# Two-layer decoder trunk on one Trainium2 core: retrieval routing decoded two heads at a time, its lists in SBUF and its scratch in PSUM, with operand splits queued behind the norm and 16 chunks in the queries

## The chip, the core and the metric

The kernel runs on one core of one Trainium2 chip. The metric is the device time of one execution in microseconds (us). A core has engines with queues of their own, each of which runs its instructions in order: PE (matrix products, into PSUM), DVE (vector work), ACT (functions and casts), POOL (a second, slower vector engine) and SP (which issues transfers). SBUF is the working memory. PSUM is a small memory of eight banks to which PE writes. An instruction that needs the result of another engine waits on a semaphore, and whatever stands behind it on its own engine waits too.

## The reference

Each of two layers mixes tokens, attends to 256 memory tokens, and then runs a retrieval over 16384 single-neuron experts, each step followed by a residual and a layer norm. The change lies in the retrieval (512 tokens, 8 heads, 128 keys on each of two sides, 16 kept):

```python
qry = (x @ wq).reshape(B, S, PEER_HEADS, PEER_QDIM)
s1 = jnp.einsum('bshc,nc->bshn', qry[..., :PEER_HALF], k1)
s2 = jnp.einsum('bshc,nc->bshn', qry[..., PEER_HALF:], k2)
v1, i1 = lax.top_k(s1, PEER_TOPK)
v2, i2 = lax.top_k(s2, PEER_TOPK)
cand = (v1[..., :, None] + v2[..., None, :]).reshape(...)
sc, ci = lax.top_k(cand, PEER_TOPK)
expert = take(i1, ci // 16) * N_KEYS + take(i2, ci % 16)
gate = softmax(sc)
out = einsum(gate * gelu(einsum(x, u[expert])), v[expert])
```

## The kernel before

The sum over chosen experts is not gathered for the first three of the four blocks of 128 tokens (384 tokens). There the kernel computes all 16384 experts, in 128 **chunks** of 128 experts. A chunk on the first side is 24 products of 128 x 384 on PE (`Peer.u_chunk`), followed on ACT by a gelu (L1219). On the second side (`Peer.dense`) its activations are multiplied by a dense row of gates (`coef`, L1240) and six blocks of products are added up in PSUM. The fourth block of tokens is gathered row by row beside that. Full precision products are made of three passes (`mm3`, L230 to L232) over a high and a low part of each operand: `split` casts the high part on ACT (L225) and subtracts for the low part on DVE or POOL (L226).

In each layer five stages touch the change.

- **Norm.** `out_proj_ln` ends with the layer norm of the last token block. `rstd` (L296) takes a logarithm and an exponential on ACT (L299, L300) and some short DVE work, `layer_norm` scales on DVE (L327), and PE transposes the result (L281). The splits of the first weights and chunks stand in the queues of ACT and POOL around it.
- **Queries** (`queries`, L777). For each head PE projects the queries (`proj`), then runs one chunk, then the scores against the keys (L806), which ACT copies to SBUF (L807). From the second head on, the low parts of the weights are subtracted on POOL (`weng`). DVE meanwhile runs `route` (L868): for each head two times four lists of 128 scores, then four lists of 80 candidates. Each list is a call of `top16`: a maximum of eight (L858), its indices (L860), a replacement (L862), and the same for the next eight (L864, L866). Sixteen short operations and three long ones (L922, L925, L929) then decode the expert's number. The best values of the first side, all indices and most of the decode's operands lie in one PSUM bank (`ps`); a second bank (`pi`) takes the shifts. `main` and `routes` are generators, and `weave` writes their code in turn by the costs that they yield. A scheduler sets the final order on each engine.
- **QUERY** is 20: after the last scores PE goes on with chunks, and the low part of a chunk is subtracted on POOL up to that number, on DVE behind it.
- **Gate rows** (`gate_rows`, L937, called from `body`, L1083). Routing must be complete. For each of three token blocks PE transposes the experts' numbers (L950) and the gates (L954). For every four tokens DVE (and ACT in one of four) makes one-hot rows (L965, L970), POOL multiplies them by the gates (L967), PE multiplies the two (L974), ACT copies the result (L975), and SP sends the rows to memory (L981). Chunks are woven in: EARLY (3) before, then AHEAD - c - LATE less EARLY, where c counts the chunks already done, and LATE (5) behind the last row. Thirty chunks (AHEAD) are thus complete when the dense stage begins.
- **Dense.** It reads the gate rows back from memory, and PE's products follow each other until the end of the layer.

`al` gives a tile of SBUF from an arena of pages; a page that was used before makes its new user wait for the old one. `bank()` hands out the eight PSUM banks in the same manner. `peer.more` allots rows for the activations.

Of the kernel before, what the change touches and what calls it, by code (L numbers as in the profile page):

```python
# [21 lines left out]
NT = S // 128  # L22
# [10 lines left out]
DT = 384  # L33
GT = 32
AHEAD = 30
QUERY = 20
EARLY = 3
LATE = 5
PF = 3
TAIL = 4  # L40
ROWS = 7
# [140 lines left out]
class K:  # L182
# [113 lines left out]
    def rstd(self, out, var, scale, eps, t, v):  # L296

        nc = self.nc
        nc.scalar.activation(t, var, AF.Ln, scale=scale, bias=eps)  # L299
        nc.scalar.activation(t, t, AF.Exp, scale=-0.5)  # L300
        nc.vector.tensor_scalar(v, var, scale, eps, op0=OP.mult, op1=OP.add)
        nc.vector.tensor_mul(out, t, t)
        nc.vector.tensor_mul(out, out, v)
        nc.vector.tensor_scalar(out, out, -0.5, 1.5, op0=OP.mult, op1=OP.add)
        nc.vector.tensor_mul(out, out, t)
# [471 lines left out]
    def queries(self, l, xT, peer, X, xs):  # L777

        nc, a = self.nc, self.a
        kk = self.al((2, NK))  # L780
        nc.sync.dma_start(kk, a["keysT"][l])
        sc = {}

        def proj(h):
            w = self.weights() if h else self.weights(0)
            q = []
            for b in ([0, 1],) if h == 0 else ([0], [1]):
                bks = [self.bank() for _ in b]
                emit(self.fm_proj(w, b, xT, bks, None if h else 0))
                for bk in bks:  # L790
                    q.append(self.al((S,)))
                    nc.scalar.copy(q[-1], bk)
            if h == 0:
                self.wahead(2, 1)
                self.weng = nc.gpsimd
            w.free()
            return q

        def scores(h, q):
            sc[h] = self.al((NT, 2, NK))  # L800
            for t2 in range(2):
                bk = self.bank((128, 2, 2, NK))
                for tt in range(2):
                    o = slice((2 * t2 + tt) * 128, (2 * t2 + tt + 1) * 128)
                    for i in range(2):
                        nc.tensor.matmul(bk[:, tt, i, :], q[i][:, o], kk[:, i, :], start=True, stop=True)  # L806
                nc.scalar.copy(sc[h][:, 2 * t2:2 * t2 + 2], bk)  # L807
            self.fr(*q)

        def main():  # L810

            for h in range(1, H):
                q = proj(h)
                yield 10.9
                peer.u_chunk()
                yield 4.2
                scores(h, q)
                yield 1.7
                for _ in range(1 if h < H - 1 else QUERY - peer.c):
                    peer.u_chunk()  # L820
                    yield 4.2

        def routes():
            for h in range(H):
# [43 lines left out]
    def route(self, h, sc, ga, ef):  # L868


        nc = self.nc
        ta, tb, sh = self.al((512,)), self.al((NT, NC)), self.al((2 * NT, 4, TOPK))
        ps, pi = self.bank(), self.bank((128, 2 * NT, 4, TOPK))

        def part(t, o, *s):
            return t[:, o:o + int(np.prod(s))].rearrange(
                "p (t n) -> p t n" if len(s) == 2 else "p (t i n) -> p t i n", t=s[0],
                **({} if len(s) == 2 else dict(i=s[1])))

# [3 lines left out]
        m = part(ps, 256, NT, TOPK).bitcast(U32)  # L883
        r = part(ps, 320, NT, 2, TOPK)
        e1 = part(ps, 448, NT, TOPK).bitcast(U32)
        v2 = part(ta, 0, NT, TOPK)
        i8 = ta[:, 64:96].bitcast(U8)
        q = part(ta, 128, NT, TOPK).bitcast(U32)
        d = part(ta, 192, NT, TOPK)
        e2 = part(ta, 256, NT, TOPK).bitcast(U32)  # L890
        tv = ga[:, :, h, :]
        for i, v in enumerate((v1, v2)):
            self.top16([(sc[:, t, i, :], v[:, t, :], ix[:, t, i, :]) for t in range(NT)])
            yield 4.3
        self.fr(sc)

        nc.vector.tensor_copy(i8, ps[:, 64:192].bitcast(U32))

        s1 = [128, NT, 7, 8]
        nc.vector.tensor_add(tb[:, :, 0:16], v1[:, :, 0:1].to_broadcast([128, NT, 16]), v2)  # L900
        nc.vector.tensor_add(tb[:, :, 16:72].rearrange("p t (a b) -> p t a b", a=7),
                             v1[:, :, 1:8, None].to_broadcast(s1), v2[:, :, None, 0:8].to_broadcast(s1))
        nc.vector.tensor_add(tb[:, :, 72:80], v1[:, :, 8:16], v2[:, :, 0:1].to_broadcast([128, NT, 8]))
        yield 0.8
        self.top16([(tb[:, t, :], tv[:, t, :], ti[:, t, :]) for t in range(NT)])
        yield 3


        nc.vector.tensor_scalar(q, ti, 120, None, op0=OP.bitwise_and)
# [6 lines left out]
        nc.vector.tensor_add(r[:, :, 1, :], r[:, :, 1, :], d)  # L916


        shape = [128, 2 * NT, 4, TOPK]
        si, su = pi.bitcast(I32), sh.bitcast(U32)  # L920
        r = r.rearrange("p t i k -> p (t i) k")
        nc.vector.tensor_sub(si, self.lanes[:, None, :, None].to_broadcast(shape),  # L922
                             r[:, :, None, :].to_broadcast(shape))
# [4 lines left out]
        en = part(ps, 320, NT, 2, TOPK).bitcast(U32)  # L928
        nc.vector.tensor_reduce(en.rearrange("p t i k -> p (t i) k"), su.rearrange("p a w k -> p a k w"),  # L929
                                axis=AX.X, op=OP.max)  # L930
        nc.vector.tensor_scalar(e1, en[:, :, 0, :], 24, None, op0=OP.logical_shift_right)
        nc.vector.tensor_scalar(e2, en[:, :, 1, :], 24, None, op0=OP.logical_shift_right)
        nc.vector.scalar_tensor_tensor(ef[:, :, h, :], e1, float(NK), e2, op0=OP.mult, op1=OP.add)
        self.fr(ta, tb, sh)
        yield 4

    def gate_rows(self, tb, ga, ef, dram, stages):  # L937

# [144 lines left out]
    def body(self, out):  # L1083
# [19 lines left out]
        for l in range(L):  # L1103
# [272 lines left out]
```

## Time and profile before

| | value |
|---|---|
| median of 3 runs | 3532.67 us (3530.05 to 3540.63) |
| the profiled execution | 3532.14 us, of which the span is 3530.4 us |
| PE busy | 3417.4 us (97% of the span) |
| DVE busy | 2570.0 us (73%) |
| ACT busy | 1431.2 us (41%) |
| POOL busy | 1136.0 us (32%) |

The span runs from the first to the last instruction of the execution. Both layers have the same form: in the first the queries lie at 485 to 690 us, the gate rows at 690 to 810 us and the dense stage at 810 to 1690 us; in the second at 2245, 2450 and 2565 us. Below, a timeline row gives the start, the length, the engine, the line, the operation with its tiles and shape, and in brackets how long the engine had been idle before and what ended that. PE's records of one product overlap the next, so one reads starts, not lengths, where records follow each other.

### The profile page before, as it was taken

The page shows a single profiled execution, that of the slowest core. Times are in us where ns is not written, and L with a number is a line of the kernel's source. Part 1 is how long each engine was busy: PE and PEld are TensorE (multiplying, and loading weights), DVE is VectorE, ACT ScalarE, POOL GpSimd, SP SyncE. Part 2 cuts the span into 40 slices and gives each one's busy share as a digit, 9 for nine tenths or more (in the row PEclk, how much of TensorE's full clock was granted, in tenths as well). Part 3 has the DMA queues.
Part 4 walks back from the last instruction along what each step waited for, and adds up shares of the span by engine and source line. Part 5 has one row for each costly group of instructions (what it writes and reads, how often), then busy time and mean ns, then how long its engine had stood idle before and what let it go on. Part 6 is the DMA issues. An engine that isn't in the chain of part 4 may idle for free.

```text
span 3530.4 us, 49767 instructions
## 1 busy us (share of the span) xinstructions
PE 3417.4 (97%) x18546; PEld 3022.8 (86%) x18546; DVE 2570.0 (73%) x5006; ACT 1431.2 (41%) x2411; POOL 1136.0 (32%) x821
## 2 busy tenths in 40 slices
PE   9999999899999999999999999997899999999998
PEld 7679789789999999998876788897899999999987
DVE  4676469996777777778746754699867777777787
ACT  5553332483333333334346532324833333333332
POOL 0110043283444343345101100433824443434450
PEclk9999999999999999999999999999999999999999
DMA  3242232259988888889612322322598888888894
GB/s 147 61 137 77 91 108 77 79 234 346 317 297 293 300 296 295 302 294 339 216 36 70 131 73 92 108 67 90 245 348 311 295 305 289 304 296 291 302 327 149
DMA packets 280579, 744.42 MB, mean 211 GB/s; under 512 B 21648, under 2 KB 120464, under 8 KB 277264
## 3 DMA queue, kind: packets, MB, share of 16 engines
q1 hardware_dynamic: 206608, 472.76, 38.8%
q0 software_dynamic: 73728, 268.47, 21.8%
q8 instruction: 146, 2.39, 0.3%
q14 instruction: 97, 0.79, 0.1%
HBM read 685.57 MB, written 55.57 MB: 210 GB/s over the span
## 4 chain that ended last, share of the span: by engine, by line
PE 81%; DVE 12%; issue 3%; ACT 2%; POOL 1%; DMA 1%; DVEq 0%; SPq 0%; POOLq 0%; ACTq 0%
PE bk L230 24%; PE bk L231 23%; PE bk L232 23%; PE bk L974 5%; DVE bk L866 2%; DVE bk L860 1%; DVE plain L862 1%; PE bk L771 1%; DVE parts L226 1%; PE bk L742 1%; PE bk L572 1%; PE bk L528 1%; DVE plain L327 1%; DVE plain L858 1%; DVE plain L864 1%
## 5 line engine op out<-in xcount | busy, mean ns | idle before, releaser
L232 PE MATMUL bk<-parts 128*128 128x384 f32 (+1 forms) x3746 | 1350.6, 361 | 4.2 <-DVE parts L226 4.2
L231 PE MATMUL bk<-parts 128*128 128x384 f32 (+2 forms) x3752 | 1333.3, 355 | 0.0
L230 PE MATMUL bk<-parts 128*128 128x512 f32 (+1 forms) x3554 | 1276.1, 359 | 0.7 <-ACT parts L225 0.7
L226 DVE TENSOR_TENSOR parts<-plain,parts 128x1024 fp32r<-128x1024 f32 (+2 forms) x747 | 730.0, 985 | 445.4 <-issue 363.9
L225 ACT CAST parts<-plain 128x1024 fp32r<-128x1024 f32 (+2 forms) x787 | 656.2, 863 | 717.1 <-PE bk L231 629.0
L232 PEld LDWEIGHTS bk<-parts 128*128 128x128 f32 x3746 | 704.1, 188 | 73.3 <-DVE parts L226 6.6
L231 PEld LDWEIGHTS bk<-parts 128*128 128x128 f32 x3752 | 706.5, 188 | 63.6
L230 PEld LDWEIGHTS bk<-parts 128*128 128x128 f32 x3554 | 669.0, 188 | 63.4 <-ACT parts L225 1.1
L1002 POOL DMA_INDIRECT mid<-peer_v,plain x256 | 377.4, 1474 | 494.4 <-DVE mid L1025 377.4
L1002 POOL DMA_INDIRECT mid<-peer_u,plain x256 | 363.9, 1421 | 530.6 <-DVE plain L1037 378.7
L230 PE MATMUL bk<-parts,mid 128*128 128x512 f32 (+2 forms) x912 | 349.5, 386 | 11.1 <-ACT mid L225 7.6
L1219 ACT ACTIVATE plain<-bk 128x384 f32<-128x384 f32 x256 | 125.4, 490 | 571.4 <-PE bk L232 571.4
L1037 DVE SCALAR_TENSOR_TENSOR plain<-mid,plain 128x1024 f32<-128x1024 f32 x256 | 329.0, 1285 | 3.4
L231 PE MATMUL bk<-parts,mid 128*128 128x512 f32 (+2 forms) x912 | 325.8, 358 | 1.5 <-DVE parts L226 1.5
L1025 DVE SCALAR_TENSOR_TENSOR mid<-mid,plain 128x1024 f32<-128x1024 f32 x256 | 303.4, 1220 | 3.3 <-DMA mid<-peer_u,plain 3.3
L226 POOL TENSOR_TENSOR parts<-plain,parts 128x1024 fp32r<-128x1024 f32 x40 | 99.4, 2490 | 526.6 <-ACT parts L225 507.8
L232 PE MATMUL bk<-parts,mid 128*128 128x512 f32 (+2 forms) x720 | 252.0, 351 | 0.0
L225 ACT CAST mid<-plain 128x1024 fp32r<-128x1024 f32 x163 | 168.9, 1038 | 193.3 <-PE bk L232 84.7
L230 PE MATMUL bk<-mid,parts 128*128 128x256 f32 (+1 forms) x798 | 237.0, 297 | 0.0
L967 POOL TENSOR_TENSOR mid<-mid,mid 128x512 f32<-128x512 f32 x192 | 192.6, 1040 | 115.6 <-DVE mid L965 114.8
L232 PE MATMUL bk<-mid,parts 128*128 128x256 f32 (+1 forms) x798 | 228.9, 287 | 0.0
L230 PEld LDWEIGHTS bk<-parts,mid 128*128 128x128 f32 (+1 forms) x912 | 171.8, 189 | 56.6 <-issue 17.8
(237 smaller groups left out, 3855.2 us busy)
## 6 DMA issues: line engine op xcount, KB each, us to landing
plain<-peer_uT SPq DMA_DIRECT2D x256, 512.0 KB, 4.7
plain<-peer_v SPq DMA_DIRECT2D x256, 512.0 KB, 5.4
plain<-gates SPq DMA_DIRECT2D x64, 768.0 KB, 9.3
gates<-plain SPq DMA_DIRECT2D x22, 2048.0 KB, 6.3
plain<-w_in SPq DMA_DIRECT2D x44, 512.0 KB, 5.4
plain<-xa_wkv SPq DMA_DIRECT2D x32, 512.0 KB, 3.8
plain<-peer_wq SPq DMA_DIRECT2D x32, 512.0 KB, 4.1
plain<-w_out SPq DMA_DIRECT2D x16, 512.0 KB, 5.0
```

What stands on the lines that cost most here:

```text
L225: nc.scalar.copy(hi, src)
L226: return (eng or nc.vector).tensor_sub(lo, src, hi.bitcast(F32))
L230: nc.tensor.matmul(out, lt[0], rt[0], start=first, stop=False)
L231: nc.tensor.matmul(out, lt[0], rt[1], start=False, stop=False)
L232: nc.tensor.matmul(out, lt[1], rt[0], start=False, stop=last)
L866: nc.vector.max_index(i[:, 8:16], v[:, 8:16], s)
L967: nc.gpsimd.tensor_mul(o[:, 0], o[:, 0], st[:, 2, t:t + 4, None].to_broadcast([128, 4, NK]))
L974: nc.tensor.matmul(bk[:, k, :], o[:, 1, k, :], o[:, 0, k, :], start=True, stop=True)
L1002: nc.gpsimd.indirect_dma_start(out=t, out_offset=None, in_=self.a[n], in_offset=bass.IndirectOffsetOnAxis(ap=ei[:, s:s + 1], axis=0))
L1025: nc.vector.scalar_tensor_tensor(u, u, 1.0, x, op0=OP.mult, op1=OP.mult, accum_out=act[:, s:s + 1])
L1037: nc.vector.scalar_tensor_tensor(acc, v, act[:, s:s + 1], acc, op0=OP.mult, op1=OP.add)
L1219: k.nc.scalar.activation(g, bk[:, :DT], AF.Gelu)
```

## The change

Three things are altered.

1. `route` handles two heads in one call. The best values of both sides, all indices, and the operands q and d lie in one SBUF tile `ta` of 1024 columns; m, r and the decoded entries in a PSUM bank; the shifts in two PSUM banks, in place. Each decode operation covers 128 columns per partition where it covered 64, save the long ones, which are done once for each half.
2. The first ahead-of-time split of the next weights (`wahead` in `proj(0)`) and `peer.preload`, which loads three chunks and splits chunk 0, are issued with an `issue_after` on the last exponential of the norm.
3. QUERY goes from 20 to 16 and LATE from 5 to 4. Eleven steps of `main` are written before the weave, where it was three, with other costs in the weave; two of the activation rows are allotted later.

```diff
-QUERY = 20
+QUERY = 16
-LATE = 5
+LATE = 4
...
-        nc.scalar.activation(t, t, AF.Exp, scale=-0.5)
+        self.last_exp = nc.scalar.activation(t, t, AF.Exp, scale=-0.5)
...
             if h == 0:
-                self.wahead(2, 1)
+                with self.tc.issue_after(norm.ins):
+                    self.wahead(2, 1)
...
-            for h in range(H):
-                yield from self.route(h, sc.pop(h), peer.ga, peer.ef)
+            for h in range(0, H, 2):
+                yield from self.route(h, sc, peer.ga, peer.ef)
...
+        norm = self.last_exp
         q = proj(0)
-        peer.preload()
+        with self.tc.issue_after(norm.ins):
+            peer.preload()
...
-        peer.more(2)
+        peer.more(1)
         m = main()
         r = routes()
-        emit(take(m, 3))
-        weave((m, 6 * 12.6 + (QUERY - 2) * 4.2), (r, 8 * 16.4))
+        emit(take(m, 11))
+        weave((m, 4 * 12.6 + (QUERY - 7) * 4.2), (r, 105))
...
-        ta, tb, sh = self.al((512,)), self.al((NT, NC)), self.al((2 * NT, 4, TOPK))
-        ps, pi = self.bank(), self.bank((128, 2 * NT, 4, TOPK))
+        N = 2 * NT
+        ta, tb = self.al((1024,)), self.al((N, NC))
+        ps = self.bank()
...
-        v1 = part(ps, 0, NT, TOPK)
-        ix = part(ps, 64, NT, 2, TOPK).bitcast(U32)
-        ti = part(ps, 192, NT, TOPK).bitcast(U32)
+        v1, v2 = part(ta, 0, N, TOPK), part(ta, 128, N, TOPK)
+        ix = part(ta, 256, N, 2, TOPK).bitcast(U32)
+        ti = part(ta, 512, N, TOPK).bitcast(U32)
...
-        nc.vector.tensor_tensor(su, words[:, :, :, None].to_broadcast(shape), pi.bitcast(U32),
-                                op=OP.logical_shift_left)
+        pi = [self.bank((128, N, 4, TOPK)) for _ in range(2)]
...
+            nc.vector.tensor_tensor(su, words[:, o, :, None].to_broadcast(shape), su, op=OP.logical_shift_left)
...
+            peer.more((AHEAD + 2) // 8 - 3)
             n = AHEAD - peer.c - LATE
```

What the scheduler makes of it shows in three places. On **DVE**, at the beginning of the first layer's routing, this stood before (names: `plain` is SBUF, `bk` a PSUM bank, the words in brackets are the semaphores waited for):

```order
L226 TENSOR_TENSOR parts<-bk,parts 128x4x128 [waits Activation_49] x2
L858 MAX plain<-plain 128x8 [waits PE_49]
L858 MAX plain<-plain 128x8 x3
L858 MAX bk<-plain 128x8
L858 MAX bk<-plain 128x8 [waits DVE_49] x3
L860 MAX_INDEX bk<-bk,plain 128x8 [waits DVE_49] x4
```

and this stands there now:

```order
L226 TENSOR_TENSOR parts<-bk,parts 128x4x128 [waits Activation_49] x2
L862 MAX plain<-plain 128x8 [waits DMAHW7_49,Pool_49]
L862 MAX plain<-plain 128x8 x3
L864 MAX_INDEX plain<-plain 128x8 [waits DVE_49] x4
L866 MATCH_REPLACE plain<-plain 128x128 [waits DVE_49] x4
L868 MAX plain<-plain 128x8 [waits DVE_49] x4
```

The first maximum waited for the scores of the second head on PE, whose pages it takes. Now it waits for a load and for POOL's subtraction of the second half of the weights of head 4, whose raw page becomes part of `ta`. The four searches of indices waited each for the one ahead of it; now each waits for its own maximum, four instructions back.

On **ACT**, ahead of the transposes of the last norm, before (`mid` are halves of weights, `parts<-plain` of 128x1024 are chunks, L299 and L300 the logarithm and the exponential):

```order
L225 CAST mid_74<-plain 128x1024
L225 CAST parts<-plain 128x1024
L225 CAST mid_76<-plain 128x1024
L225 CAST parts<-plain 128x1024
L225 CAST parts<-bk 128x4x128 x2
L225 CAST mid_78<-plain 128x1024
L225 CAST parts<-plain 128x1024
L225 CAST parts<-bk 128x4x128 x2
L299 ACTIVATE ln_t<-ln_mv,eps_ln 128x1
L225 CAST parts<-plain 128x1024
L300 ACTIVATE ln_t<-ln_t 128x1
```

and now:

```order
L225 CAST mid_74<-plain 128x1024
L225 CAST parts<-plain 128x1024 x3
L225 CAST parts<-bk 128x4x128 x3
L299 ACTIVATE ln_t<-ln_mv,eps_ln 128x1
L225 CAST parts<-bk 128x4x128
L300 ACTIVATE ln_t<-ln_t 128x1
L225 CAST mid_76<-plain 128x1024
L225 CAST mid_78<-plain 128x1024
L225 CAST parts<-plain 128x1024
```

Two halves of weights and chunk 0 moved behind the exponential; the casts of three other chunks still stand ahead of it.

On **ACT** again, at the end of the first block of gate rows, before (`bk 128x128x4` are the rows of four tokens that L975 copies):

```order
L971 ACTIVATE mid_5557<-mid_5557 128x512
L975 COPY plain<-bk 128x128x4 x7
L951 COPY mid_5559<-bk 128x256
L970 ACTIVATE mid_5562<-iota,mid_5559 128x128
L955 COPY mid_5559<-bk 128x128
```

and now:

```order
L985 ACTIVATE mid_5381<-mid_5381 128x512
L989 COPY plain<-bk 128x128x4 x5
L1234 ACTIVATE plain<-bk 128x384
L225 CAST parts<-plain 128x1024
L989 COPY plain<-bk 128x128x4 x3
L965 COPY mid_5383<-bk 128x256
```

A chunk (its gelu is L1234 now) stands inside the block. Before, 23 chunks stood ahead of the first transposes (L950), one between them and the first one-hot product, one inside the second block and five behind the last row. Now it is 19, one, two in each of the three blocks, and four.

## Rows read from the trace of the kernel before

**Rows 1.** Windows: columns, then queries, a wait in them, gate rows (us).

```profile
core 0: us, PE busy (x) PEld busy (x) DVE busy (x) ACT busy (x) POOL busy (x), PEclk, DMA share, GB/s
485.00:690.00 205.00, 190.66 (x1008) 175.56 (x1006) 177.03 (x931) 66.84 (x98) 62.10 (x26) 0.98 0.25 78
628.00:636.00 8.00, 4.78 (x22) 4.59 (x23) 7.42 (x30) 4.41 (x7) 2.37 (x1) 0.79 0.00 1
693.50:804.70 111.20, 101.89 (x800) 99.71 (x801) 97.92 (x103) 93.17 (x216) 98.28 (x98) 0.94 0.55 225
```

**Rows 2.** Timeline of PE, first layer, rows with a wait (start, length, operation, [wait]).

```profile
631.22 3.68 PE L806 MATMUL bk<-plain 128*128 128x128 f32 x16 [4.19 <-ACT plain L792]
...
681.92 0.66 PE L950 MATMUL bk<-ident,mid 128*128 128x128 f32 x2 [7.22 <-DVE mid L947]
...
729.79 7.39 PE L974 MATMUL bk<-mid 128*128 128x128 f32 x47 [2.80 <-POOL mid L967]
...
799.28 5.40 PE L974 MATMUL bk<-mid 128*128 128x128 f32 x32 [2.21 <-POOL mid L967]
```

**Rows 3.** Timeline of DVE: the first and the last instruction of the routing.

```profile
500.96 0.87 DVE L858 MAX8 plain<-plain 128x8 f32<-128x128 f32 x4 [25.83 <-PE bk L806]
...
676.52 0.22 DVE L933 SCALAR_TENSOR_TENSOR plain<-bk,plain 128x64 f32<-128x64 uint32 x1
```

**Rows 4.** Timeline of POOL: the two halves of the weights of head 4.

```profile
515.85 2.40 POOL L226 TENSOR_TENSOR mid<-plain,mid 128x1024 fp32r<-128x1024 f32 x1 [5.76 <-ACT mid L225]
518.57 2.38 POOL L226 TENSOR_TENSOR mid<-plain,mid 128x1024 fp32r<-128x1024 f32 x1 [0.32 <-ACT mid L225]
```

**Rows 5.** Timeline of DVE: lists and decode of one head.

```profile
527.09 1.31 DVE L864 MAX8 bk<-plain 128x8 f32<-128x128 f32 x4
...
528.52 0.29 DVE L866 FIND_INDEX8 bk<-bk,plain 128x8 uint32<-128x128 f32 x1
...
528.93 0.29 DVE L866 FIND_INDEX8 bk<-bk,plain 128x8 uint32<-128x128 f32 x1
...
531.09 0.29 DVE L860 FIND_INDEX8 bk<-plain 128x8 uint32<-128x128 f32 x1
531.29 0.07 DVE L862 MATCH_VALUE_LOAD plain<-plain 128x8 f32 x1
...
532.32 0.87 DVE L864 MAX8 plain<-plain 128x8 f32<-128x128 f32 x4
...
541.34 0.23 DVE L914 TENSOR_TENSOR bk<-bk,plain 128x64 f32<-128x64 f32 x1
541.61 0.22 DVE L915 TENSOR_TENSOR plain<-bk,plain 128x64 f32<-128x64 uint32 x1
```

**Rows 6.** Groups by shape, DVE, 484 to 690 us (busy us, mean ns | idle).

```profile
L862 DVE MATCH_REPLACE8 plain<-plain 128x128 f32<-128x128 f32 x32 | 8.7, 276 | 0.0
L862 DVE MATCH_REPLACE8 plain<-bk,plain 128x128 f32<-128x128 f32 x32 | 8.6, 276 | 0.0
```

**Rows 7.** Timelines of POOL, then of DVE, in the norm.

```profile
453.99 9.04 POOL L226 TENSOR_TENSOR parts<-plain,parts 128x1024 fp32r<-128x1024 f32 x3 [194.05 <-ACT parts L225]
...
458.00 5.58 DVE L327 SCALAR_TENSOR_TENSOR plain<-plain,ln_r 128x512 f32<-128x512 f32 x2
...
471.60 1.41 DVE L327 SCALAR_TENSOR_TENSOR plain<-plain,ln_r 128x512 f32<-128x512 f32 x2
```

**Rows 8.** One line and a timeline row: POOL's products (ns), PE's at full pace.

```profile
L967 POOL TENSOR_TENSOR mid<-mid,mid x96: 1036/1039/1047, 692.4 to 802.4; 128x512 f32<-128x512 f32 x96
...
751.14 5.07 PE L974 MATMUL bk<-mid 128*128 128x128 f32 x44
```

**Rows 9.** Timelines of DVE, then PE, where the dense stage begins.

```profile
825.89 1.03 DVE L1240 TENSOR_TENSOR plain<-plain 128x384 f32<-128x384 f32 x2 [7.56 <-DMA plain<-gates]
826.83 1.69 DVE L226 TENSOR_TENSOR parts<-plain,parts 128x1024 fp32r<-128x1024 f32 x2
...
829.50 0.39 PE L230 MATMUL bk<-parts 128*128 128x512 f32 x1
```

More of the change, by code (lines that the diff above doesn't have):

```diff
@@ L878, in part @@
                 **({} if len(s) == 2 else dict(i=s[1])))
-        v1 = part(ps, 0, NT, TOPK)
-        ix = part(ps, 64, NT, 2, TOPK).bitcast(U32)
-        ti = part(ps, 192, NT, TOPK).bitcast(U32)
[L883 to L900, printed above, removed]
+        v1, v2 = part(ta, 0, N, TOPK), part(ta, 128, N, TOPK)
@@ new lines, in route @@
+        ix = part(ta, 256, N, 2, TOPK).bitcast(U32)
+        ti = part(ta, 512, N, TOPK).bitcast(U32)
+        q = part(ta, 640, N, TOPK).bitcast(U32)
+        d = part(ta, 768, N, TOPK)
+        i8 = ta[:, 896:960].bitcast(U8)
+        m = part(ps, 0, N, TOPK).bitcast(U32)
+        r = part(ps, 128, N, 2, TOPK)
+        for k in range(2):
+            s = sc.pop(h + k)
+            for i, v in enumerate((v1, v2)):
+                self.top16([(s[:, t, i, :], v[:, k * NT + t, :], ix[:, k * NT + t, i, :]) for t in range(NT)])
+                yield 4.3
+            self.fr(s)
@@ L901, in route @@
+        nc.vector.tensor_copy(i8, ta[:, 256:512].bitcast(U32))
+        s1 = [128, N, 7, 8]
+        nc.vector.tensor_add(tb[:, :, 0:16], v1[:, :, 0:1].to_broadcast([128, N, 16]), v2)
         nc.vector.tensor_add(tb[:, :, 16:72].rearrange("p t (a b) -> p t a b", a=7),
                              v1[:, :, 1:8, None].to_broadcast(s1), v2[:, :, None, 0:8].to_broadcast(s1))
-        nc.vector.tensor_add(tb[:, :, 72:80], v1[:, :, 8:16], v2[:, :, 0:1].to_broadcast([128, NT, 8]))
-        yield 0.8
@@ L905, in route @@
-        self.top16([(tb[:, t, :], tv[:, t, :], ti[:, t, :]) for t in range(NT)])
-        yield 3
+        nc.vector.tensor_add(tb[:, :, 72:80], v1[:, :, 8:16], v2[:, :, 0:1].to_broadcast([128, N, 8]))
+        yield 1.2
+        for k in range(2):
+            self.top16([(tb[:, k * NT + t, :], ga[:, t, h + k, :], ti[:, k * NT + t, :]) for t in range(NT)])
+            yield 3
         nc.vector.tensor_scalar(q, ti, 120, None, op0=OP.bitwise_and)
@@ L916, in route @@
         nc.vector.tensor_add(r[:, :, 1, :], r[:, :, 1, :], d)
[L919 to L923, printed above, removed]
-        words = i8.bitcast(U32).rearrange("p (a w) -> p a w", w=4)
-        nc.vector.tensor_tensor(su, words[:, :, :, None].to_broadcast(shape), pi.bitcast(U32),
-                                op=OP.logical_shift_left)
@@ L928, in route @@
[L928 to L931, printed above, removed]
-        nc.vector.tensor_scalar(e2, en[:, :, 1, :], 24, None, op0=OP.logical_shift_right)
-        nc.vector.scalar_tensor_tensor(ef[:, :, h, :], e1, float(NK), e2, op0=OP.mult, op1=OP.add)
-        self.fr(ta, tb, sh)
@@ L935, in route @@
-        yield 4
+        shape = [128, N, 4, TOPK]
+        words = i8.bitcast(U32).rearrange("p (a w) -> p a w", w=4)
+        rr = r.rearrange("p t i k -> p (t i) k")
+        pi = [self.bank((128, N, 4, TOPK)) for _ in range(2)]
+        en = part(ps, 128, N, 2, TOPK).bitcast(U32)
+        for k in range(2):
+            o = slice(k * N, (k + 1) * N)
+            nc.vector.tensor_sub(pi[k].bitcast(I32), self.lanes[:, None, :, None].to_broadcast(shape),
+                                 rr[:, o, None, :].to_broadcast(shape))
@@ new lines, in route @@
+        for k in range(2):
+            o = slice(k * N, (k + 1) * N)
+            su = pi[k].bitcast(U32)
+            nc.vector.tensor_tensor(su, words[:, o, :, None].to_broadcast(shape), su, op=OP.logical_shift_left)
+        for k in range(2):
+            su = pi[k].bitcast(U32)
+            nc.vector.tensor_reduce(en.rearrange("p t i k -> p (t i) k")[:, k * N:(k + 1) * N],
+                                    su.rearrange("p a w k -> p a k w"), axis=AX.X, op=OP.max)
+        e2 = d.bitcast(U32)
@@ L937, in gate_rows @@
+        nc.vector.tensor_scalar(en[:, :, 0, :], en[:, :, 0, :], 24, None, op0=OP.logical_shift_right)
+        nc.vector.tensor_scalar(e2, en[:, :, 1, :], 24, None, op0=OP.logical_shift_right)
+        for k in range(2):
+            o = slice(k * NT, (k + 1) * NT)
+            nc.vector.scalar_tensor_tensor(ef[:, :, h + k, :], en[:, o, 0, :], float(NK), e2[:, o],
+                                           op0=OP.mult, op1=OP.add)
+        self.fr(ta, tb)
+        yield 7
     def gate_rows(self, tb, ga, ef, dram, stages):
```

## Prediction

> **What bounds the kernel now.** I read the busy times first: PE works in 97% of the span, so only the stretches where it does not can give or take time. I then went through PE's timeline for rows with a wait. They stand in one place of each layer, between the norm and the dense stage, and the largest are in [rows 2]: 4.19 us ahead of the last scores, 7.22 us at the first transposes of the gate rows, 2.80 us at each border between token blocks, 2.21 us near the end. The windows [rows 1] say who is late. In the queries DVE has 177.03 us of 205 and PE 190.66: the routing, a chain on DVE from 500.96 to 676.74 us [rows 3], 175.8 us long, ends last, and PE fills the time with chunks until it has none (the 7.22 us). In the gate rows POOL has 98.28 us of 111.2: 96 products of 1.039 us are 99.7 us [rows 8], and PE is held to that pace. A one-hot record at PE's own pace takes 5.07 / 44 = 0.115 us [rows 8], 768 of them 88.5 us; with the one chunk inside, 92.6 of the 111.2 us. So 18.6 us of the gate rows are PE's slack, 7.8 in the waits of [rows 2], the rest hidden as slower one-hot records.
>
> One chunk costs 4.14 us: six of them lie between the last one-hot product, 799.28 + 5.40 = 804.68 us [rows 2], and the first product of the second side at 829.50 us [rows 9].
>
> The rule for the sum: the work on PE is the same before and after. Thirty chunks are done ahead of the dense stage in either kernel; they only change place. I follow the end that sets each stage.
>
> **Norm.** Two DVE instructions took 5.58 us while POOL ran three subtractions, and 1.41 us on the last token block [rows 7], so 4.2 us of the chain to PE's transposes is there to be had. The change puts one of POOL's four subtractions (chunk 0) and the casts of two halves behind the exponential; the casts of three other chunks stay ahead of it, so POOL's 9.04 us stretch stays. I take -1.5 us per layer: bounds 0 (same three subtractions, same overlap) and -4. Chunk 0 is then split later, but PE has the projection of the first head's queries ahead of it.
>
> **Routing, its length.** Per head, searches of indices that wait for each other start 528.93 - 528.52 = 0.41 us apart; one that has another instruction between starts the next 0.20 us later, plus 0.07 for the load of values, 0.27 [rows 5]. I count 13 chained of 24 in a head; the new order has none, so 13 x 0.14 = 1.8 us. Four maxima into PSUM take 1.31 us, into SBUF 0.87 [rows 5]: 0.5 us once a head. Two heads: 4.6. The decode's short instructions are 0.27 us apart [rows 5]; sixteen of them per pair become eight of twice the columns, which I put at 0.33: 16 x 0.27 - 8 x 0.33 = 1.7. From that I take off 0.4, since before the next head's lists filled gaps in the decode and a pair offers them half as often. So 5.9 us per pair, 23.6 for four, and 152 us long. Bounds: the chains alone, 4 x 4.6 = 18 (157 us); with the long decode instructions gaining as well, 30 (146 us).
>
> **Routing, its start.** This decides the sign. Before, the first maximum waits for scores on PE, and starts at 500.96. Now it waits for POOL's second half of the weights of head 4, which ends at 518.57 + 2.38 = 520.95 us [rows 4]. POOL was not behind there: it had waited 5.76 us for ACT's cast, which follows PE's projections, so nothing in the change brings it forward. The start moves by 20 us, and of the 23.6 us only 3.6 stay: the end goes from 676.7 to 673.2. Bounds 666.8 and 678 from the two lengths. PE meanwhile has four chunks less, 16.6 us, so its wait of 7.22 us at the transposes grows to some 16 or 20; that costs nothing by itself, since DVE ends last, and the chunks come back in the next term.
>
> **Gate rows.** Five more chunks stand in the three blocks, 20.7 us. The floor for PE is 88.5 + 6 x 4.14 + the two borders' 2 x 2.80 = 118.9 us, with transposes and small waits at the borders about 122, against 111.2: PE is now the bound in place of POOL's 99.7. It cannot use the slack in full, since at 8 x 0.115 = 0.92 us against 1.04 for four tokens it gains only 0.12 us per product of POOL's, some 4 us in a block of 32, and two chunks are 8.3. I take +12. Bounds +7.7 (118.9) and +20.7 (no slack used). The moved chunks' subtractions go to DVE, which has 97.92 of 111.2 us [rows 1]; five of 1.2 us fit into the longer stage.
>
> **Behind the last gate row.** One chunk less: -4.1. But it was cover. The first gates come back by a transfer for which DVE waited 7.56 us, and the first coefficient's parts end at 826.83 + 1.69 = 828.52 [rows 9], 23.8 us behind the last one-hot product. Before, the cover (five chunks and the dense stage's own first) ended at 829.50, 1.0 us later. Now it is 5 x 4.14 = 20.7 us: PE waits 3.1. A wait is followed by a slow clock: around the wait of 4.19 us the granted clock was 0.79 over 8 us [rows 1], at half for part of it, 1.7 us lost; such a wait would be new here. With what the first dense chunks may wait for late coefficients I take +2, bounds 0 and +6.
>
> **The sum.** Per layer -1.5 - 3.5 + 12 - 4.1 + 3.1 + 2 = +8.0; two layers +16. The profiled execution took 3532.1 us, 0.5 less than the median, so 3548 us.
>
> **A rule against the trace.** Searches and replacements take a list and its best values, both in SBUF in the new kernel. Where before the values were in PSUM they took 276 ns, where in SBUF 276 ns [rows 6], with POOL busy for 62.10 of the 205 us [rows 1]: no contention is seen. The short additions of [rows 7] did suffer, and the change's three additions per pair (first-side values now in SBUF) are of that kind: at POOL's share of 30% and at most 2.4 us a hit, 12 additions cost between 0 and 10 us per layer, most likely 1 to 2; that is in the upper bound of the routing's end.
>
> The Trainium skill (SBUF — State Buffer, Who interferes with whom) says that a DVE instruction with two SBUF inputs contends with a POOL instruction that reads SBUF, and that the loser waits for the whole instruction. The norm's rows agree with it; the replacements' rows do not, for their kind. By the rule alone the lists would stall too, which is rival C.
>
> **Rivals.**
> A, faster: the start is not held. If the pages of the tile are free by 501 us (POOL gets to head 4's weights early, or another page is taken at run time), the end of the routing comes at 653, 20 us sooner, and each layer gains 20 - 8 = 12: 3508 us. For it: the routing really is shorter. Against: the semaphore is named in the order, and POOL's time hangs on PE's projections. 0.11.
> B, no change: the routing takes 146 us (end 667, -10), the gate rows use nearly all slack (+9), the rest as above (-1.5 - 4.1 + 3.1 + 2): -1.5 per layer, 3529; with one of the two, about 3537. For it: decode of a pair may alternate its two halves; 18.6 us of slack are there. 0.27.
> C, slower by contention: of POOL's 26 subtractions in the queries some 20 lie inside the routing; if each held the lists for half its 2.4 us, the routing would be 24 us longer, 3596 us. Against it stand the equal 276 ns. 0.04.
> D, the norm part does nothing, since three subtractions still overlap the norm: +1.5 per layer, 3551. It is inside the forecast.
>
> **Chances.** Forecast 0.58 (3538 to 3566), A 0.11, B 0.27, C 0.04. A measurement of this kernel can tell about 0.3%, 10.6 us, from no change: 3522 to 3543. Faster: A, and 0.04 of B: 0.15. Within: 0.22 of B and 0.06 of the forecast: 0.28. Slower: 0.57. The range for 8 in 10 leaves out A, C and the ends of the others: 3526 to 3567 us, of which the terms' bounds alone give about -6 to +35 us around 3532.
>
> **What would show it.** In the new trace: the first L862 row of the routing near 521 us (at 501: A); its last row near 673; PE's wait at L964 of 12 to 20 us; the span from first to last one-hot product about 123 us against 111; a wait of some 3 us on DVE's split ahead of the first product of the dense stage; the wait of 4.19 us ahead of the last scores gone or moved. I would be wrong if the routing were under 146 us, or if the gate rows swallowed the five chunks, which would show as one-hot records at 0.115 us throughout and a stage under 118 us.

## The result and the profile after

The changed kernel takes 3562.78 us (median of 4 runs, 3559.88 to 3568.19), the kernel before 3534.63 us beside it: a ratio of 1.0080, 95% interval 1.0060 to 1.0101. That is 28 us slower, where 3548 us was forecast (+16): inside the range and the way right, but the forecast size is a little over half of the measured one. The profiled execution has a span of 3561.7 us.

The windows of the changed kernel, from the start of the first one-hot product to that of the last, then behind the first product of the dense stage:

```profile
core 0: us, PE busy (x) PEld busy (x) DVE busy (x) ACT busy (x) POOL busy (x), PEclk, DMA share, GB/s
680.50:808.10 127.60, 119.79 (x917) 118.53 (x918) 104.43 (x108) 98.88 (x226) 97.36 (x97) 0.93 0.52 207
833.00:900.00 67.00, 63.67 (x296) 57.05 (x297) 49.12 (x77) 21.98 (x33) 17.39 (x11) 0.92 0.93 296
```

Counted so, the gate rows took 110.9 us before (111.2 in [rows 1], which go to the last product's end) and take 127.6. Behind the dense start PE is idle in places, and the granted clock is 0.92 on the mean.

The timeline of PE, rows with a wait, answers [rows 2]:

```profile
634.18 0.69 PE L230 MATMUL bk<-parts 128*128 128x384 f32 x1 [4.11 <-DVE bk L939]
668.57 0.66 PE L964 MATMUL bk<-ident,mid 128*128 128x128 f32 x2 [14.87 <-DVE mid L961]
...
723.49 11.63 PE L988 MATMUL bk<-mid 128*128 128x128 f32 x80 [2.80 <-POOL mid L981]
...
767.19 6.59 PE L988 MATMUL bk<-mid 128*128 128x128 f32 x32 [2.80 <-POOL mid L981]
...
833.03 0.50 PE L230 MATMUL bk<-parts 128*128 128x512 f32 x1 [3.75 <-ACT parts L225]
876.16 0.69 PE L232 MATMUL bk<-parts 128*128 128x384 f32 x1 [3.17 <-DVE parts L226]
```

The transposes (L964) come at 668.57 us, 13.3 earlier than in [rows 2], although PE stands idle for 14.87 us ahead of them. The wait of 4.19 us ahead of the last scores is gone; one of 4.11 us, which ends with a reduction of the decode (L939), has come behind them. The gain is gone by the dense stage's first product, 833.03 us where it was 829.50 [rows 9]; two waits follow there that the kernel before did not have in this place, 3.75 and 3.17 us.

The routing's first and last rows on DVE ([rows 3]), the start of the second half of head 4's weights on POOL ([rows 4]), and one pair of searches ([rows 5]):

```profile
518.08 0.87 DVE L862 MAX8 plain<-plain 128x8 f32<-128x128 f32 x4 [45.65 <-POOL mid L226]
518.93 0.28 DVE L864 FIND_INDEX8 plain<-plain 128x8 uint32<-128x128 f32 x1
...
519.19 0.28 DVE L864 FIND_INDEX8 plain<-plain 128x8 uint32<-128x128 f32 x1
...
664.21 0.35 DVE L946 SCALAR_TENSOR_TENSOR plain<-bk,plain 128x64 f32<-128x64 uint32 x2
...
515.65 2.40 POOL L226 TENSOR_TENSOR mid<-plain,mid 128x1024 fp32r<-128x1024 f32 x1 [0.33 <-ACT mid L225]
```

As read from the order, the routing starts when POOL has ended that subtraction (518.05). Searches are 0.26 us apart, and the routing is 146.5 us long.

Taking the first layer step by step, by differences of starts in the two timelines (before to after, us):

| step | forecast | measured |
|---|---|---|
| first scores (norm) | -1.5 | -2.9 (483.6 to 480.7) |
| transposes, beyond that (routing) | -3.5 | -10.4 (681.9 to 668.6) |
| first to last one-hot product | +12 | +16.7 (110.9 to 127.6) |
| chunks behind the last row | -4.1 | -4.1 (21.1 to 17.0) |
| wait at the dense start | +3.1 | +3.8 |
| chunks 31 to 40, beyond that wait | +2 | +8.6 |
| sum | +8 | about +12 |

The second layer has +15.7 from its first scores to chunk 40. The remaining 3.6 us of the 31.3 between the two spans lie in the second layer's mixer and cross-attention, where the change touches the norm alone. They are scatter: from chunk 40 to the second layer's first scores the fourteen profiles of this case take 1336.0 to 1343.9 us, and three with the same code in that stretch (the kernel before, e8, e11) 1338.1, 1341.3 and 1338.6.

### The profile page after: what moved, and what is told of

It is laid out like the page before. It is cut to its first block, busy times and chain, and to the rows that moved or that the text cites. A ratio compares the mean times of both kernels' runs of the same rounds, so it can differ in the third digit from the quotient of the medians.

```text
span 3561.7 us, 49560 instructions
## 1 busy us (share of the span) xinstructions
PE 3426.4 (96%) x18546; PEld 3030.3 (85%) x18546; DVE 2528.8 (71%) x4902; ACT 1428.6 (40%) x2411; POOL 1120.6 (31%) x813
## 5 line engine op out<-in xcount | busy, mean ns | idle before, releaser
L226 DVE TENSOR_TENSOR parts<-plain,parts 128x1024 fp32r<-128x1024 f32 (+2 forms) x755 | 738.3, 987 | 476.1 <-issue 375.8
L1234 ACT ACTIVATE plain<-bk 128x384 f32<-128x384 f32 x256 | 125.5, 490 | 604.4 <-PE bk L232 604.3
L226 POOL TENSOR_TENSOR parts<-plain,parts 128x1024 fp32r<-128x1024 f32 x32 | 80.8, 2531 | 477.8 <-PE bk L231 387.8
```

The costliest lines, as they stand in the source:

```text
L226: return (eng or nc.vector).tensor_sub(lo, src, hi.bitcast(F32))
L1234: k.nc.scalar.activation(g, bk[:, :DT], AF.Gelu)
```

## The experiments

Ratios are against the kernel before on the same chip. "Chunks 31 to 40" is the time from the end of the 31st to the end of the 40th group of 24 products of 128x384 on PE's timeline: 74.8 us in the kernel before, 87.2 in the changed one.

**Placement undone.** QUERY and LATE as before, pairs and norm part kept:

```diff
-QUERY = 16
+QUERY = 20
-LATE = 4
+LATE = 5
```

> The changed kernel with QUERY back at 20 and LATE at 5, so that only the routing by pairs and the norm part are left; the chunks stand as in the kernel before (23 ahead of the transposes, one ahead of the first one-hot product, one in the second block, five behind). Theory (the loss comes from where the chunks stand): gate rows from first to last one-hot product about 111 us as before, not 128; no waits at the dense start; the transposes at 668 to 672 us against 681.9 before: 10 to 13 us per layer less than the kernel before, 3507 to 3515 us. Rival (the routing by pairs itself lengthens the gate rows and the dense start, by its larger tiles and the later activation rows): 128 us of gate rows and the waits stay, 3550 us or more.

3513.13 us, ratio 0.9929 (0.9903 to 0.9954). Windows, and the one row of PE at the transposes:

```profile
681.20:792.10 110.90, 101.56 (x796) 99.46 (x797) 97.92 (x103) 93.12 (x216) 98.07 (x98) 0.94 0.55 224
817.00:900.00 83.00, 83.00 (x421) 75.57 (x421) 71.14 (x104) 29.52 (x42) 28.01 (x20) 1.00 0.98 336
...
669.36 0.66 PE L964 MATMUL bk<-ident,mid 128*128 128x128 f32 x2 [5.69 <-DVE mid L961]
```

Gate rows are back at 111.0 us, PE is busy throughout at the dense start, and the transposes keep their 12.5 us. The two constants cost the changed kernel all of its loss and some 20 us more. The routing by pairs and the norm part together are a gain. QUERY also sets which engine subtracts a chunk's low part and a cost in the weave; no run parts these from the chunks' place.

**One constant.** LATE alone:

```diff
-LATE = 4
+LATE = 5
```

> The changed kernel with LATE back at 5 (QUERY stays 16): five chunks in the three blocks of gate rows where it was six, five behind the last row where it was four. Theory (one chunk too little cover for the transfer of the first gates): the last one-hot product comes about 4 us earlier, the first product of the dense stage needs no wait (3.75 us before), and the second wait some 43 us later (3.17 us, for gates again) and the slow clock behind both shrink or go: 6 to 12 us per layer less, 3539 to 3551 us. Rival (the early dense stage is bound by the transfers in any case): the waits stay, the chunk only changes place, 3560 us.

3530.8 us, ratio 0.9985 (0.9973 to 0.9996): 32 us less than the changed kernel, where 12 to 24 were expected. The window of the gate rows, then PE's rows:

```profile
681.00:797.00 116.00, 112.22 (x892) 110.28 (x893) 103.74 (x107) 96.74 (x224) 100.58 (x97) 0.99 0.56 227
...
716.87 0.33 PE L968 MATMUL bk<-ident,plain 128*128 128x128 f32 x1 [0.21 <-ACT mid L965]
730.71 6.62 PE L988 MATMUL bk<-mid 128*128 128x128 f32 x56 [0.37 <-ACT mid L985]
...
862.54 0.69 PE L232 MATMUL bk<-parts 128*128 128x384 f32 x1 [2.31 <-DVE parts L226]
```

One chunk fewer took 11.5 us from the gate rows (127.6 to 116.1). With six chunks in the weave instead of seven, one falls on each border, from between the transposes of L964 and L968 on: the waits there, 0.64 and 2.80 us at the first border of the changed kernel, become one of 0.21 us, with another of 0.37 us ten us behind it, and the granted clock over the stage is 0.99 instead of 0.93. The wait at the first product of the dense stage is gone; the second is there with 2.31 us.

**Border and cover apart.** LATE stays 4, and one more chunk goes ahead of the transposes, so that six are left to weave:

```diff
-EARLY = 3
+EARLY = 4
```

> The changed kernel with EARLY 4 where it was 3, LATE stays 4: one more chunk goes ahead of the first transposes (where PE waits 14.87 us), and the six that are left in the weave fall on the borders between token blocks, as in e2_late5. Theory (a third of the loss is the gate rows with idle borders and the slow clock behind each, the rest the missing cover at the dense start): gate rows 116 us instead of 127.6, as in e2_late5; the dense start keeps its waits, since four chunks follow the last row: chunk 31 to chunk 40 takes 84 to 87 us, 3543 to 3548 us. Rival 1 (all of e2_late5's gain came from the gate rows): 3531. Rival 2 (all from LATE): 3560.

3539.95 us, ratio 1.0011 (1.0002 to 1.0021). Gate rows 116.1 us, as with LATE 5; chunks 31 to 40 in 87.0 us, close to the changed kernel's 87.2, with both waits, each shorter, and a third:

```profile
822.81 0.50 PE L230 MATMUL bk<-parts 128*128 128x512 f32 x1 [2.45 <-ACT parts L225]
864.51 0.44 PE L232 MATMUL bk<-parts 128*128 128x384 f32 x1 [1.95 <-DVE parts L226]
...
880.81 0.51 PE L231 MATMUL bk<-parts 128*128 128x512 f32 x1 [3.66 <-DVE parts L226]
```

So of the 32 us, some 23 come from the chunk that leaves the rows for the place ahead of the transposes and from the borders that the rest then cover, and 9 from the fifth chunk behind the rows.

**The cover without pairs.** The kernel before, LATE alone:

```diff
-LATE = 5
+LATE = 4
```

> The kernel before with LATE 4 alone: one chunk of the five behind the last gate row goes into the rows. Theory (the waits at the dense start come from the missing cover, whatever the routing): the first product of the dense stage waits about 3 to 4 us, chunk 31 to chunk 40 takes 84 to 88 us instead of 74.7, gate rows grow by up to 4 us: 4 to 12 us per layer, 3543 to 3558 us. Rival (the waits come with the pair routing, its pages or the later activation rows): dense start as before, 3530 to 3537 us.

3544.89 us, ratio 1.0027 (1.0015 to 1.0038). Gate rows 112.1 us with three chunks on the borders; chunks 31 to 40 in 83.2, with these waits and a third of 1.44 us:

```profile
827.19 0.50 PE L230 MATMUL bk<-parts 128*128 128x512 f32 x1 [0.73 <-ACT parts L225]
869.02 0.45 PE L232 MATMUL bk<-parts 128*128 128x384 f32 x1 [3.48 <-DVE parts L226]
```

The waits at the dense start do not need the routing by pairs.

**The held start.** The first pair's tile of lists is taken ahead of the weights:

```diff
+        self.first = self.al((1024,))
         emit(take(m, 11))
...
-        ta, tb = self.al((1024,)), self.al((N, NC))
+        ta, tb = self.first or self.al((1024,)), self.al((N, NC))
```

> The changed kernel with one edit: the first pair's tile of 1024 columns is taken from the arena ahead of the weights of heads 1 to 4, so that its pages were not just those of head 4's weights, and the first maximum waits for the copy of the scores alone. Theory (the held start eats the shorter routing): the first L862-type row falls from 518 to about 497 us, the routing keeps its 145 us and ends some 20 us earlier, and PE's wait at the gate rows' transposes (14.87 us) goes to 0 to 2, since PE's own chunks then end last: 13 to 17 us per layer less than the changed kernel, 3528 to 3537 us. Rival (the routing's end does not matter, PE's placement of chunks alone makes the loss): no change, 3560 us or more.

3560.52 us, ratio 1.0075 (1.0046 to 1.0104): no change. The routing starts at 484.4 us and ends at 664.3. Who DVE waited for in it (total, times, longest):

```profile
DVE plain L905 <- PE bk L807: 32.4, 1, 32.4
DVE plain L863 <- ACT plain L808: 17.7, 2, 11.8
```

The next tile, that of the candidates (L905), held it in place of the first: the candidates start at 541.99 us, where they started at 540.39 in the changed kernel. The run answers nothing on the start; the next does.

**Both tiles free**, with LATE 5:

```diff
+        self.first = self.al((1024,)), self.al((2 * NT, NC))
         emit(take(m, 11))
```

> LATE 5 as in e2_late5, and the first pair's two tiles (the lists' and the candidates') are taken ahead of the weights, so that neither start nor candidates of the first pair wait for pages. Theory after e1_free_start: a second tile held the routing there (32.40 us of idle before the first candidates), so nothing was free; and behind that hold stands a floor that no tile moves, the last scores (625.5 us) plus the last pair's second half, some 27 us of lists, candidates and decode: end at about 657 us where e2_late5 has 665.0, transposes 8 us earlier, 3530.8 - 16 = 3515 us. Rival (the held start never mattered, scores alone set the end at 664): 3531 us, end at 664 to 665.

3509.56 us, ratio 0.9929 (0.9912 to 0.9946), 21 less than LATE 5 alone. The routing starts at 485.8 and ends at 655.5:

```profile
DVE plain L863 <- ACT plain L808: 32.0, 4, 11.9
DVE plain L905 <- POOL mid L226: 6.0, 1, 6.0
...
485.81 0.49 DVE L863 MAX8 plain<-plain 128x8 f32<-128x128 f32 x2 [11.95 <-ACT plain L808]
...
659.48 0.66 PE L966 MATMUL bk<-ident,mid 128*128 128x128 f32 x2 [11.14 <-DVE mid L963]
```

Started 33 us earlier it ends 9.5 us earlier. Behind the held start stands the arrival of the scores: of the 32.0 us that DVE waits for them 11.95 lie ahead of the first row, 20.0 inside the routing, for the second to fourth head. Another 6.0 go to the second tile, which still waits for POOL. All of this is over at 559 us, and from there DVE waits for nothing until the routing ends, so the last scores (625.6 us) do not hold it. My 20 us for a free start (rival A) was twice what it gave.

**Earlier scores.** With both tiles free, QUERY 20 and LATE 5, one chunk less between two heads:

```diff
-                for _ in range(1 if h < H - 1 else QUERY - peer.c):
+                for _ in range(0 if h < H - 1 else QUERY - peer.c):
...
-        emit(take(m, 11))
-        weave((m, 4 * 12.6 + (QUERY - 7) * 4.2), (r, 105))
+        emit(take(m, 7))
+        weave((m, 4 * 12.6 + (QUERY - 4) * 4.2), (r, 80))
```

> QUERY 20 and LATE 5 as in e4_query20_late5, both tiles of the first pair free as in e5, and one chunk less between two heads' scores (it follows the last scores instead), so that the last scores come 6 x 4.1 us earlier, at about 601 us. Theory (scores arrive every 20.6 us per head, a pair of lists takes 36.5 us, so with a free start the scores set the routing's pace): routing ends at 630 to 640 us, PE never waits at the transposes, which then come when PE has done its 23 chunks, at about 664 us against 669.4: 3513 - 11 = 3502 us. Rival (DVE is the bound in any order): routing's end and time as in e4, 3513 us.

3527.76 us, ratio 0.9983 (0.9973 to 0.9993). A miss: the last scores begin at 599.6 us, as meant, and the routing ends at 668.8.

```profile
DVE plain L863 <- ACT plain L808: 41.7, 4, 22.1
DVE plain L863 <- PE bk L807: 6.1, 1, 6.1
```

Inside the routing DVE waited 36.0 us for scores, 20.0 in e5, in one place 22.1 us, until 584.63. In the order that the scheduler made of the new weave the rest of a decode that had begun at 562.06 (L915) stands behind the lists for which it waited, and goes on only at 611.91 (L916); whether it could have gone on earlier is not shown. The edit changed two things, the scores' time and DVE's order, so it does not decide whether the scores set the pace.

**Free tiles and the old placement**, QUERY 20 and LATE 5:

> The routing by pairs with the chunks where they stood before (QUERY 20, LATE 5, as in e4_query20_late5) and both tiles of the first pair free, as in e5_both_free_late5. Theory (three separate costs in the change: placement at the gate rows, cover at the dense start, held tiles): the routing ends at about 656 us, so PE's 23 chunks end last and the transposes come at 663 to 665 us without a wait, gate rows 111 us, dense start as before: 5 us per layer less than e4, 3499 to 3504 us. Rival (the gain of e5 was its gate rows' borders, not the free tiles): 3513 us.

3502.48 us, ratio 0.9908 (0.9891 to 0.9924). PE's wait at the transposes is 1.67 us, and chunks 31 to 40 take 74.7 us. In this profile the first scores come late, at 487.9 us (481.1 in e4); counted from there, the transposes come 184.3 us later, 4.0 us sooner than in e4.

```profile
672.16 0.41 PE L966 MATMUL bk<-ident,mid 128*128 128x128 f32 x2 [1.67 <-DVE mid L963]
```

**QUERY 19** on top of that:

> As e9 with QUERY 19: 22 chunks ahead of the transposes, three woven in, at the beginning of each block of gate rows, five behind. Theory (a chunk is cheap where it covers a border's wait, which e2_late5 and e8_before_late4 showed, and where it does not make PE late for the transposes): transposes at about 660 us, gate rows 112 us, 2 to 3 us per layer less than e9: 3494 to 3499 us. Rival (PE is the bound everywhere, so a chunk costs 4.1 us wherever it stands): as e9.

3518.8 us, ratio 0.9958 (0.9941 to 0.9974): another miss. The gate rows take 110.0 us with three chunks in them, as hoped, but the dense start has a wait again, and chunks 31 to 40 take 82.7 us, though five chunks stand behind the last row:

```profile
664.50 0.66 PE L966 MATMUL bk<-ident,mid 128*128 128x128 f32 x2 [5.26 <-DVE mid L963]
...
854.51 0.69 PE L232 MATMUL bk<-parts 128*128 128x384 f32 x1 [5.89 <-DVE parts L226]
...
852.76 0.56 DVE L1257 TENSOR_TENSOR plain<-plain 128x384 f32<-128x384 f32 x1 [5.87 <-DMA plain<-gates]
```

DVE waited for gates being read back, 42 us behind the first product of the dense stage. So the second wait is not a matter of the number of late chunks alone. In the runs without it, chunks stood at the first block's head and inside the second block, none in the third; but e6 had that placement too, and 80 us. SP's order of loads and reads differs among these kernels; which transfer is late, and behind what, I have not settled.

**Lists in SBUF, one head at a time.** The kernel before, with one more tile of 64 columns (`tc`), and the copy that reads the indices turned to `ta`:

```diff
-        v1 = part(ps, 0, NT, TOPK)
-        ix = part(ps, 64, NT, 2, TOPK).bitcast(U32)
-        ti = part(ps, 192, NT, TOPK).bitcast(U32)
+        v1 = part(ta, 320, NT, TOPK)
+        ix = part(ta, 384, NT, 2, TOPK).bitcast(U32)
+        ti = part(tc, 0, NT, TOPK).bitcast(U32)
```

> The kernel before, one head at a time, with the best values of the first side and all indices in SBUF instead of the PSUM bank; everything else stays. Theory (the chained searches of indices in PSUM are three quarters of the routing's saving, 2.3 us a head): the routing ends when the last scores plus one head's work allow, some 15 to 20 us earlier than 676.7, PE's 7.22 us at the transposes go, and with it part of the 4.19 us at the last scores: 8 to 11 us per layer, 3512 to 3519 us. Rival (decoding two heads in one instruction is what saves): routing 170 us or more and 3530 to 3535 us.

3501.68 us, ratio 0.9909 (0.9892 to 0.9926). The routing starts at 500.0 as before and ends at 654.3:

```profile
654.09 0.22 DVE L934 SCALAR_TENSOR_TENSOR plain<-bk,plain 128x64 f32<-128x64 uint32 x1
...
665.14 0.38 PE L951 MATMUL bk<-ident,mid 128*128 128x128 f32 x2
...
521.21 0.28 DVE L866 FIND_INDEX8 plain<-plain 128x8 uint32<-128x128 f32 x1
...
521.47 0.28 DVE L866 FIND_INDEX8 plain<-plain 128x8 uint32<-128x128 f32 x1
```

PE goes into the transposes without a wait, and searches are 0.26 us apart as in the pairs. This placement of the lists gives the time that the pairs give with free tiles (e9): the routing is 154.3 us long, 21.5 less than before. The pairs, as changed, took 7.8 us more off and paid for them with the held tiles.

**The norm part.** On the kernel before, and on e11 (in both as in the change: `issue_after` around `wahead` and `preload`):

> The kernel before with one part of the change: the splits of the next weights and of chunk 0 issued behind the norm's last exponential. Theory (one POOL subtraction fewer beside the norm's scaling): the first scores come 2 to 3 us earlier in each layer, as in the changed kernel (480.7 against 483.6 us), 3527 to 3530 us. Rival (the three subtractions that stay take all of it, and the earlier scores came from elsewhere): 3534 us, first scores at 483.6.

3533.62 us, ratio 0.9995 (0.9981 to 1.0008). The first scores of the first layer come at 482.3 us instead of 483.6.

> e11_before_lists and the norm part of the change: the kernel before with lists in SBUF, one head at a time, and the splits of the next weights and of chunk 0 behind the norm's last exponential. Theory (in e3_norm_alone the first scores came only 1.3 us earlier in the first layer, and the whole 0.05% earlier): 1 to 2.5 us per layer, 3497 to 3500 us; the transposes come when PE has done its 23 chunks, so an earlier norm carries through. Rival (the norm part gains nothing, because three of POOL's subtractions still overlap the norm): 3501 to 3502 us, first scores at 482.7 us as in e11.

3500.0 us, ratio 0.9906 (0.9890 to 0.9923), the first scores 0.7 us earlier than in e11. The two intervals of e11 and e12 lie on each other. Alone the norm part is worth about 1 us a layer or nothing that a measurement tells.

## Why the prediction was right, and where it was not

**The way was right, for a reason that was half wrong.** The prediction said of the routing's start: "This decides the sign." It does not. With the start held as in the change (518.4 us), e4 is 0.7% faster than the kernel before. With both tiles freed e5 gains 21 us over e2, less than the 28 that the change loses; the change with both constants and both tiles free was not run. The hold was read rightly from the order, and its time from [rows 4] (520.95 forecast, 518.1 measured, with the norm 2.9 earlier). The step that failed is the free routing that I set against the held one (rival A): I had it start at 501, wait for nothing and end at 653 us, 20 ahead of the held one. In e5 it started at 485.8, waited 20.0 us for scores and 6.0 for a tile, and ended at 655.5; that this is near 653 is luck. The held one ended at 664.6, not 673.2, so 9.5 us are left between the two (against e2). What decides the sign is the two constants: e4 against the change is 50 us.

**The size came within the range in part by luck.** In the first layer norm and routing gave 8.3 us more than forecast, and the gate rows and the dense start cost 12 us more; most of the two errors cancel.

**Routing's length**: 152 us forecast, 146.5 measured, at the bound of 146. The searches are 0.26 apart as taken from [rows 5] (0.27). Part of the rest is a row that my sum left out, though the bound of 146 allowed for the long decode instructions: the reduction at the decode's end, eight of 1.05 us each before, reading SBUF, and 0.70 each now, reading PSUM, 2.8 us per layer.

**Gate rows**: +12 forecast, +16.7 measured, within its bounds of 7.7 and 20.7. The argument of pace held: PE could not use the slack. What I left out is that a wait at a border is followed by a slow clock, though I had priced just that for the wait at 631 us, and [rows 1] gives 0.94 for this very stage. I took PE's missing pace there for slack; at 0.94 some 7 us of the 111.2 were slow clock, which, as I now read it, cost little while POOL set the pace. My floor of 118.9 us with the 0.93 of the changed kernel, some 9 us of 127.6, comes to about 128 (an estimate), and 127.6 were measured. The stage ran at 0.93 with uncovered borders and at 0.99 with covered ones (e2), where one chunk fewer, 4.1 us of work, made it 11.5 us shorter.

**Dense start**: the first wait was 3.75 us against 3.1, from the cover, as e2 and e7 show by putting it back and leaving it out (its size is not fixed: 2.45 us in e7, 0.73 in e8). But the term behind it, +2, measured +8.6: a second wait for gates, 3.17 us, and slow clock behind both. This is the term that most of the missing half belongs to, together with the gate rows; it came with the changed placement of the chunks (e8 has it without pairs, e4 has pairs without it), but e6, with the old placement, took 80.0 us there too. By what path that transfer is delayed is open.

**Norm**: -1.5 forecast, -2.9 seen in the profile after; alone it gave 1.3 us in the first layer and nothing measurable in time, so rival D stands as far as the time tells. Three subtractions of POOL still overlap the norm, as the order said, and a fourth now meets the scaling of the last token block: its two instructions took 3.55 us (466.55 us), 1.41 in [rows 7].

**Contention**: short instructions in SBUF did meet POOL. The shape groups of the changed kernel for the replacement, the reduction and two operations with both ends in SBUF (busy us, mean ns):

```profile
L866 DVE MATCH_REPLACE8 plain<-plain 128x128 f32<-128x128 f32 x64 | 16.9, 275 | 0.0
L939 DVE TENSOR_REDUCE bk<-bk 128x128 uint32<-128x512 uint32 x8 | 5.6, 695 | 0.1
L900 DVE CAST plain<-plain 128x256 uint8<-128x256 uint32 x4 | 3.2, 798 | 0.0
L906 DVE TENSOR_TENSOR plain<-plain 128x64 f32<-128x64 f32 x4 | 3.1, 768 | 0.0
```

and the two that were held, with POOL's rows beside them:

```profile
536.92 2.33 DVE L900 CAST plain<-plain 128x256 uint8<-128x256 uint32 x1
541.13 2.42 DVE L906 TENSOR_TENSOR plain<-plain 128x64 f32<-128x64 f32 x1
...
536.71 2.39 POOL L226 TENSOR_TENSOR parts<-plain,mid 128x1024 fp32r<-128x1024 f32 x1 [0.31 <-ACT mid L225]
540.94 2.53 POOL L226 TENSOR_TENSOR parts<-plain,parts 128x1024 fp32r<-128x1024 f32 x1 [1.84 <-ACT parts L225]
```

Of the four additions of L906 one took 2.42 us and the median 0.22; of the four casts of L900 one took 2.33, and of the four scalar operations of L913 one 1.62 (median 0.21). Each of the three began while a subtraction of POOL ran and ended within 0.2 us of its end. That is 5.6 us in the first layer: 2.2 for the additions, which I had priced at "most likely 1 to 2" in bounds of 0 to 10, and 3.4 for two kinds that I had not priced. The replacements stayed at 275 ns with all operands in SBUF ([rows 6]: 276): rival C fell. Their values come by an instruction of their own ([rows 5], MATCH_VALUE_LOAD); the prediction took list and values for two inputs of one instruction, and no row bears that out. The Trainium skill (SBUF — State Buffer, Who interferes with whom) names both additions with two SBUF inputs and copies or casts as able to contend with POOL; these rows agree.

**Rival B** had one of its two conditions: the routing did reach 146 us, and the gate rows did not give up their slack.

## What to carry to other kernels

Filler work on the engine that is the bound is not free to move. In these runs a piece was worth its place when it covered a wait (a border between blocks, a transfer that comes back), and cost more than itself when it left one open, because the slow clock behind the wait came on top. When a chain starts late, ask what would bind it if it did not; the time to be had is the distance to that second limit, not the delay. And test the parts of a bundle alone: here one part of the change, lists in SBUF, gave 0.9% by itself, and two constants of the same change cost more than that.

## What the runs showed of the hardware

A reduction of 128x512 to 128x128 that reads every sixteenth word took 1.05 us with its input in SBUF and 0.70 us (the group of L939 above) with it in PSUM; its row in the kernel before:

```profile
L929 DVE TENSOR_REDUCE bk<-plain x8: 1014/1050/1069, 522.6 to 674.9; 128x128 uint32<-128x512 uint32 x8
```

Searches of indices that follow each other into PSUM started 0.41 us apart and into SBUF 0.26, with almost the same length of the single instruction (0.29 and 0.28). By the order, each into PSUM waited for the one ahead of it, so I put the 0.15 us down to the wait; no run has such a wait with the results in SBUF.

Waits of 3.75 and 3.17 us on PE were each followed by a stretch with part of its time at the lower of the two clock levels:

```profile
833.00:843.00 10.00, 9.84 (x40) 8.29 (x41) 6.63 (x11) 4.50 (x7) 0.00 (x0) 0.83 0.96 327
876.00:886.00 10.00, 9.84 (x36) 9.30 (x37) 10.00 (x18) 0.00 (x0) 2.99 (x2) 0.69 0.72 232
```

The slow clock cost about three quarters as much again as the waits: chunks 31 to 40 of the changed kernel lost 12.4 us with 6.9 us of waits.
